# Row factors of the first block by a product, rows loaded first, and one set of weights loaded a phase earlier

## The chip, the cores and the metric

The kernel runs on one core of one Trainium2 chip. The metric is the device time of one execution in microseconds; several runs are made and their median is taken. A profile is a further execution of the same program, recorded by the hardware profiler: it has a time of its own, and a span from its first to its last instruction. The engines are named as in the profile: PE (TensorE matmuls) and PEld (its weight loads), DVE (VectorE), ACT (ScalarE), POOL (GpSimd) and SP (SyncE, which here only issues DMAs).

## The reference

One layer of a hybrid decoder, in float32, on 4096 new tokens and on 64 sample tokens (8 sequences of 8), all of width 1024:

```python
h = _rmsnorm(x, g_pre)
z = h @ w_in                       # 1024 x 2816
cb, cc, ch, cg, q, k, v, ag, mq, mg = _split_cols(z)
...                                # gated conv3 | sliding-window attention | cross-attention, each times silu(gate)
y = jnp.concatenate([out_a, out_b, out_c], axis=-1) @ w_out
return x + _rmsnorm(y, g_post), new_conv, new_k, new_v
```

with

```python
def _rmsnorm(x, g):
    xf = x.astype(jnp.float32)
    r = lax.rsqrt(jnp.mean(xf * xf, axis=-1, keepdims=True) + RMS_EPS)
    return (xf * r).astype(x.dtype) * g
```

So each token (a row of x) has one factor r. What follows is about how these factors reach the tiles that need them.

## The kernel before

**The projection.** The 4160 tokens (the 64 sample tokens first) are cut into 8 blocks of 520. The 22 groups of 128 columns of `w_in` are handled in three phases (`PHASES`): phase 0 has 8 groups as 4 pairs, phase 1 the 8 groups of the convolution, phase 2 the other 6. In the code phases count from 0; what the title of the change calls phase 1 and 2 are indices 0 and 1. A phase runs over the blocks; a block is a list of steps, and in a step PE multiplies the weights of every pair of the phase with one operand: 48 matmul instructions, each operand and weight split into a high and a low part of a reduced type (`split`, `w_split`: a cast on ACT, then a subtraction on DVE). In phase 0 the first two blocks (`PLAIN_BLOCKS`) have 8 plain steps each (`plain_block`); all later blocks have 7 steps with the sums of a Strassen-like scheme (`PRODUCTS`: A11, A12, S2, S3, S1, S4, A22 with B11, B21, T2, T3, T1, B22, T4). S1 to S4 are sums of weights, formed during blocks 3 to 6 of phase 0 and kept in DRAM (`sd`).

**Order.** Phase 0 is in an order written out by hand for all five engines, up to the first step of phase 1 (`in_order`); after that the framework's scheduler orders. In a step the jobs that belong beside it (loads, splits, sums, squares) are put between the products of its four pairs, an equal share after each: `upto = len(jobs) * (q + 1) // 4`. An engine works its instructions in order; a load waits on its queue (SP's or POOL's) until its tile is free and its source is written, and everything behind it on that queue waits too.

**The row factors.** A row tile (`nat`, 104 tokens in natural layout) is loaded by SP (`row_load`), squared and summed on ACT (`row_step`, L259); five tiles make one block. After the fifth, POOL raises the mean to the power -1/2 (L266). The operands are transposed (features on partitions, tokens along the free axis), so the factors are needed along the free axis, the same in each partition. For that POOL stores them to DRAM (`rowd`, L270), and some steps later SP loads them back, broadcast over 128 partitions (`rows_load`, L234); `row_spreads` counts the steps between. The first two blocks are multiplied without factors, and their results are scaled afterwards (`z_rows`, L597). The third block (index 2) does it another way: `rows_diag` makes five diagonal matrices of its factors (DVE, L277), `rows_product` multiplies them with a matrix of ones on PE (L286), which gives the factors in every partition, and ACT copies them out of PSUM (L288). The diagonals' tile is lent from the pool of row tiles (`rows_place`), which has two buffers; a row tile uses one of them or, early on, a slot of the weights that is still free.

**The queue of loads.** `row_queue` issues the row loads and factor loads that are due. In a plain step it comes after the step's loads of operands (`x_of`, L221); in the later steps of phase 0 (`next_block`) it comes after the loads of the next block's operands and after a sum on DVE.

**From phase 0 to phase 1.** `SWITCH` says in which step the next phase's weights are loaded (`next_loads`) and split into their slots (`next_fills`). A11, A12 and S2 are loaded and split in the last block of phase 0; S3, S1, S4 and A22 are loaded in the first steps of phase 1, into the temporary tiles (`temp`) of the new phase.

**Afterwards** come the attention, in chunks of 256 tokens (line numbers from 960 on), the output projection, and the sample tokens. `mix_s` holds the sample's mixed outputs, first written in phase 1; `pv` (L1123) holds masked weights of the window attention.

Of the kernel before, what the change touches and what calls it, by code (L numbers as in the profile page):

```python
# [8 lines left out]
F32 = mybir.dt.float32  # L9
# [3 lines left out]
ALU = mybir.AluOpType  # L13
AX = mybir.AxisListType

P = 128
D = 1024
# [3 lines left out]
NS = 64  # L21
NB = 8
NT = 4096 + NS
HW = 260
# [19 lines left out]
PLAIN_BLOCKS = 2  # L44
# [7 lines left out]
def hybrid_layer(ctx: ExitStack, tc: tile.TileContext, a: dict):  # L52
    nc = tc.nc
    TE, V, S, G, DMA = nc.tensor, nc.vector, nc.scalar, nc.gpsimd, nc.sync

    const = ctx.enter_context(tc.tile_pool(name="const", bufs=1))
    tiny = ctx.enter_context(tc.tile_pool(name="tiny", bufs=3))
# [11 lines left out]
    convw = const.tile([P, 2, 3], F32, name="convw")  # L69

    zs = const.tile([P, 14, NS], F32, name="zs")
    mix_s = const.tile([P, 8, NS], F32, name="mix_s")

    rowd = [tc.dram_tile([2 * HW], F32, name=f"rowd{b}") for b in range(NBLK)]
    hd = [{o: tc.dram_tile([P, KH, HW], F32, name=f"hd{b}_{o}") for o in ("B12", *(o for _, o in PRODUCTS))}
# [149 lines left out]
    RG = 104  # L225
# [24 lines left out]
    def row_step():  # L250

        j = sq[0]
        if j == 5 * NBLK:
            return
        b, i = divmod(j, 5)
        if i == 0:
            nat["r"] = tiny.tile([P, 8], F32, tag="r", name=f"r{b}", bufs=2)
        r, t = nat["r"], nat.pop(j)
        S.activation(t[:RG], t[:RG], AF.Square, accum_out=r[:RG, i : i + 1])  # L259
        if j in (10, 11) or j >= 14:  # L260
            row_loads.append(after_nat[0])
            after_nat[0] += 1
        sq[0] += 1
        if i == 4:
            G.tensor_scalar(r[:RG, 0:5], r[:RG, 0:5], 1.0 / D, EPS, op0=ALU.mult, op1=ALU.add)
            G.tensor_tensor(r[:RG, 0:5], r[:RG, 0:5], mhalf[:RG, 0:5], op=ALU.pow)  # L266
            if b == PLAIN_BLOCKS:
                nat["first"] = r
                return
            G.dma_start(rowd[b].rearrange("(i p) -> p i", p=RG), r[:RG, 0:5])  # L270
            row_spreads[b] = 2 if b < PLAIN_BLOCKS else 4

    def rows_diag():

        t = nat["diag"]
        for i in range(5):
            V.tensor_scalar(t[:, RG * i : RG * (i + 1)], ident[:RG, :RG], nat["first"][:RG, i : i + 1], None, op0=ALU.mult)  # L277

    def rows_place():
        nat["diag"] = natp.tile([P, D], F32, tag="nat", name="diag")[:RG, : 2 * HW]  # L280

    def rows_product():

        acc = pa2.tile([P, 2, 512], F32, tag="y", name="rows_y", bufs=2)[:, :, :HW]
        for half in range(2):
            TE.matmul(acc[:, half], ones[:RG], nat["diag"][:, HW * half : HW * half + HW], start=True, stop=True)  # L286
        rows[PLAIN_BLOCKS] = natp.tile([P, 2 * HW], F32, tag="rb", name="rb_first")
        S.copy(rows[PLAIN_BLOCKS].rearrange("p (a n) -> p a n", a=2), acc)  # L288

    def row_queue():  # L290

# [232 lines left out]
    def next_block(ph, b, p):  # L524
# [9 lines left out]
        if p < 3 and ph == 0:  # L534
            jobs.append(lambda: t_sum(ph, b, f"T{p + 2}"))
        if ph == 0:
            jobs.append(row_queue)
            if 1 <= p < 6:
                jobs.append(row_step)
        if p == 1 and nph == 1 and nb < PLAIN_BLOCKS:  # L540
# [52 lines left out]
    def z_rows(b, row):  # L593

        def one(z):
            z = z.rearrange("p a b n -> p a (b n)")
            V.tensor_tensor(z, z, rows[b].unsqueeze(1).to_broadcast([P, 2, 2 * HW]), op=ALU.mult)  # L597
        return [lambda z=zz[b][q][row]: one(z) for q in range(2)]

    def plain_jobs(b, s):  # L600
# [14 lines left out]
            (0, 4): lambda: [*parts(0, "B22"), *fills(0, "S3", "S1"), *row, *fills(0, "S4"), *row],  # L615
            (0, 5): lambda: [*sums(1, 0), *row, *sums(1, 1), *fills(1, "S2", "S3"), *row],
            (0, 6): lambda: [*parts(1, "B11"), *row, *fills(1, "S1", "S4"), *sums(3, 0), *row],
            (0, 7): lambda: [*row, *fills(3, "S2", "S3")],
            (1, 0): lambda: [*parts(1, "B21"), *z_rows(0, 1), *row, *row],
            (1, 1): lambda: [*z_rows(0, 0), *done(0, 1), *row, *row],  # L620
            (1, 2): lambda: [*parts(1, "B12"), *row, rows_place, *done(0, 0), *fills(3, "S1")],
            (1, 3): lambda: [lambda: rows_diag(), *sums(2, 0), *row],
            (1, 4): lambda: [lambda: rows_product(), *parts(1, "B22"), *sums(2, 1), *fills(2, "S2"),
                             *gains(2, "B11", "B21"), *row],
            (1, 5): lambda: [*fills(2, "S3", "S1", "S4"), *scales(2, "B11"), *row],
            (1, 6): lambda: [*gains(2, "B12"), *scales(2, "B21", "B12"), *row],
# [187 lines left out]
    def next_fills(o):  # L814
        return [lambda q=q: next_fill(1, q, o) for q in range(4)]
# [9 lines left out]
    def wo_split(j):  # L825
# [4 lines left out]
    last = NBLK - 1  # L830
    SWITCH = {(0, last - 1, 6): lambda: next_loads("A11", True),
              (0, last, 1): lambda: [*next_fills("A11"), *next_loads("A12"), *next_loads("S2", True)],
              (0, last, 3): lambda: [*next_fills("A12"), *next_fills("S2")],
              (1, 0, 0): lambda: next_loads("S3"),
              (1, 0, 1): lambda: next_loads("S1"),
              (1, 0, 2): lambda: [*next_fills("S3"), *next_loads("S4")],
              (1, 0, 3): lambda: [*next_fills("S1"), *next_loads("A22")],
              (1, 0, 4): lambda: next_fills("S4"),
              (1, 0, 5): lambda: next_fills("A22")}

    def input_projection():
        for i, (ph, b, p) in enumerate(steps):
# [135 lines left out]
    class Chunk:  # L978
# [105 lines left out]
        def window_unit(self, i, kvh, steps):  # L1084
# [34 lines left out]
            p3 = pt.rearrange("p (h q) -> p h q", h=4)  # L1119
            if not first:  # L1120

                pv = wp.tile([P, 512], F32, tag="pv", name=f"wpv{b}_{kvh}")
                G.affine_select(pv.rearrange("p (h q) -> p h q", h=4), p3, pattern=[[0, 4], [-1, P]], compare_op=ALU.is_gt,  # L1123
                                fill=0.0, base=0, channel_multiplier=1)
                steps.append((self.vts[i], pv))
# [390 lines left out]
```

## Time and profile before

| | |
|---|---|
| median of 3 runs | 1638.24 us (1634.79 to 1640.45) |
| profiled execution, its own time | 1641.21 us |
| its span | 1639.5 us |
| mean granted clock of TensorE | 0.987 |
| PE, PEld, DVE, ACT, POOL busy | 97%, 85%, 72%, 48%, 21% of the span |
| DMA | 305.89 MB, mean 187 GB/s |

How the views read: the page gives busy times of the engines and groups of instructions; the stretches view gives, for chosen times, each engine's busy time and its number of instructions, the clock granted to TensorE (1.00 is full) and the mean share of 16 DMA engines at work; the timeline lists instructions of an engine with start, duration, line, operation, tile written and tiles read, and in brackets how long the engine had been idle and what ended that; the waits view sums who waited for whom; the chain of waits is followed back from the last instruction, and its rows have a start, a duration and what ran. A row "SPq" is an instruction of SP's queue, that is a DMA being issued; the issue ends when the DMA is handed over, not when it has landed. Buffer numbers are partly left out of names: `xl5B` is an operand of block 5, `w_0S` a weight of pair 0, `c` the accumulators in PSUM, `z` the results.

### The profile page before, as it was taken

Reading aid. Unit: us, or ns where it says so; the run is one execution under the profiler, and the core shown is the slowest. Engines: PE = TensorE matmul, PEld = TensorE weight load, DVE = VectorE, ACT = ScalarE, POOL = GpSimd, SP = SyncE. Lnnn points to the kernel's source line nnn. Section 1 sums busy time; section 2 is a strip of 40 time slices with the busy share of each in tenths; the row PEclk is TensorE's granted clock in tenths of the full one; section 3 lists DMA queues with packets and bytes.
Section 4 is the critical chain, followed back from the end, with each engine's and each line's share of the span. In section 5 each row is a group of like instructions: output and inputs, shape, how many; then the busy total and the mean of one; then the engine's idle time right before and its main releaser. Section 6 shows DMA issues by size and latency. Waiting matters only on the chain.

```text
span 1639.5 us, 29607 instructions
## 1 busy us (share of the span) xinstructions
PE 1585.3 (97%) x11095; PEld 1399.6 (85%) x11095; DVE 1182.2 (72%) x2126; ACT 788.9 (48%) x2022; POOL 345.8 (21%) x590
## 2 busy tenths in 40 slices
PE   9899999999999999999999979999999999999997
PEld 9899999999999999998999955777777777777766
DVE  6578878898988777974766777666777677676733
ACT  6566655465222222443434456555555555555522
POOL 0122222220000000000000025444333443443210
PEclk9999999999999999999999989999999999999999
DMA  9979999867544333789667699666666676665152
GB/s 250 185 204 213 278 253 254 293 201 268 179 169 170 118 120 126 274 254 286 216 216 253 235 278 155 127 151 139 139 143 147 150 155 142 139 143 112 54 188 90
DMA packets 175252, 305.89 MB, mean 187 GB/s; under 512 B 31109, under 2 KB 104581, under 8 KB 175077
## 3 DMA queue, kind: packets, MB, share of 16 engines
q1 hardware_dynamic: 128213, 227.02, 44.7%
q0 software_dynamic: 46176, 75.92, 24.0%
q8 instruction: 88, 1.44, 0.4%
q10 hardware_dynamic: 720, 1.05, 0.2%
q14 instruction: 55, 0.45, 0.1%
HBM read 196.81 MB, written 108.12 MB: 186 GB/s over the span
## 4 chain that ended last, share of the span: by engine, by line
PE 49%; DVE 21%; DMA 10%; ACT 8%; issue 7%; POOL 4%; SPq 0%; ACTq 0%; DVEq 0%; POOLq 0%
PE c L345 35%; PE y L1339 6%; ACT sm L1106 5%; DMA nat<-in_x_p 3%; DVE sm L1112 3%; DVE sm L1096 2%; DVE wmx L1098 2%; PE wt L1116 2%; POOL xp L1061 1%; DVE yn L1346 1%; PE wo L976 1%; PE xs L1053 1%; DVE mix L1080 1%; DVE xr L1357 1%; DVE ml L1322 1%
## 5 line engine op out<-in xcount | busy, mean ns | idle before, releaser
L1339 PE MATMUL y<-wo,mh 128*128 128x512 f32 (+1 forms) x1072 | 351.3, 392 | 2.3 <-DVE mh L1316 1.4
L352 DVE TENSOR_TENSOR z<-c,z 128x520 f32<-128x520 f32 (+1 forms) x308 | 194.1, 645 | 83.6 <-PE c L345 82.8
L1339 PEld LDWEIGHTS y<-wo,mh 128*128 128x128 f32 x1072 | 201.0, 189 | 44.4 <-issue 4.1
L1339 PE MATMUL y<-wo,ml 128*128 128x512 f32 (+1 forms) x520 | 203.2, 391 | 1.1 <-DVE ml L1322 1.1
L1106 ACT ACTIVATE sm<-sm,wnm 128x128 f32<-128x128 f32 x256 | 99.9, 391 | 77.3 <-DVE wnm L1100 77.3
L1339 PEld LDWEIGHTS y<-wo,ml 128*128 128x128 f32 x520 | 98.5, 189 | 16.5 <-DVE ml L1322 1.6
L998 POOL DMA_DIRECT2D kst<-qd x64 | 38.9, 622 | 249.6 <-DMA qd<-z 182.4
L1123 POOL TENSOR_SCALAR_AFFINE_SELECT wpv<-wpt 128x512 f32<-128x512 f32 x62 | 39.6, 638 | 223.3 <-ACT wpt L1118 222.5
L1093 PE MATMUL ws<-kst,q 128*128 128x256 f32 x512 | 79.7, 296 | 0.5 <-ACT sm L1095 0.4
L1054 DVE TENSOR_REDUCE xmx<-xs 128x2 f32<-128x512 f32 x64 | 44.2, 690 | 42.3 <-PE xs L1053 42.2
L1057 ACT ACTIVATE xp<-xs,xnm 128x256 f32<-128x256 f32 x128 | 59.4, 469 | 31.4 <-DVE xnm L1055 25.3
L1095 ACT COPY sm<-ws 128x256 f32<-128x256 f32 x128 | 44.4, 372 | 59.2 <-PE ws L1093 56.1
L711 POOL CAST wmask<-negs 128x256 uint8<-128x256 f32 x1 | 1.4, 1419 | 324.9 <-DVE w_0S L173 324.9
L1061 POOL TENSOR_SCALAR xp<-xp,xrd 128x256 f32<-128x256 f32 x128 | 61.7, 488 | 36.6 <-DVE xrd L1058 34.0
L1347 ACT ACTIVATE y<-y 128x512 f32<-128x512 f32 (+1 forms) x66 | 38.8, 587 | 62.1 <-DVE yn L1346 62.0
L1093 PEld LDWEIGHTS ws<-kst,q 128*128 128x128 f32 x512 | 66.2, 192 | 2.4 <-ACT sm L1095 0.8
L1346 DVE TENSOR_TENSOR yn<-y,gpost 128x512 f32<-128x512 f32 (+1 forms) x66 | 45.1, 683 | 30.2 <-PE y L1339 29.8
L1357 DVE SCALAR_TENSOR_TENSOR xr<-yn,yst,xr 128x1024 f32<-128x1024 f32 (+2 forms) x34 | 42.5, 1253 | 27.9 <-POOL yst L1353 27.9
L1116 PEld LDWEIGHTS wt<-ident,sm 128*128 128x128 f32 x256 | 28.1, 144 | 38.0 <-ACT xp L1057 19.4
L259 ACT ACTIVATE nat<-nat 104x1024 f32<-104x1024 f32 x40 | 42.3, 1057 | 31.0 <-DMA nat<-in_x_p 31.0
L1066 PEld LDWEIGHTS xt<-ident,xp 128*128 128x128 f32 x256 | 29.1, 141 | 32.9 <-PE wo L976 10.5
L1116 PE MATMUL wt<-ident,sm 128*128 128x128 f32 x256 | 42.3, 289 | 15.3 <-DVE xrd L1058 8.1
(959 smaller groups left out, 5134.3 us busy)
## 6 DMA issues: line engine op xcount, KB each, us to landing
q<-qd POOLq DMA_DIRECT2D x64, 384.0 KB, 5.9
mix<-md SPq DMA_DIRECT2D x16, 1024.0 KB
xr<-in_x_p SPq DMA_DIRECT2D x32, 512.0 KB
nat<-in_x_p SPq DMA_DIRECT2D x39, 416.0 KB
o_yp<-xr SPq DMA_DIRECT2D x31, 512.0 KB
md<-th POOLq DMA_DIRECT2D x48, 260.0 KB, 6.2
qd<-zh SPq DMA_DIRECT2D x48, 260.0 KB
qd<-z SPq DMA_DIRECT2D x48, 260.0 KB
```

The source lines that it names most:

```text
L345: TE.matmul(bank[:, :HW], l, r, start=first and i == 0, stop=last and i == 3 * KH - 1)
L352: add = lambda dst, other: V.tensor_tensor(dst, c, other, op=ALU.add)
L1057: S.activation(p[:, i, :], s[:, i, :], AF.Exp, bias=nm[:, i : i + 1], scale=SCALE, accum_out=den[:, i : i + 1])
L1061: G.tensor_scalar(p[:, i, :], p[:, i, :], rd[:, i : i + 1], 0.5, op0=ALU.mult, op1=ALU.mult)
L1093: TE.matmul(s3[:, hh, :], self.q[:, 4 + 2 * (2 * half + hh) + kvh, i * P : i * P + P], self.kst[:, 2 * kvh + part, i * P : i * P + 2 * P], ...
L1095: S.copy(sm[:, 2 * half : 2 * half + 2, :], s3[:, :, P : 2 * P])
L1106: S.activation(sm[:, hh, :], sm[:, hh, :], AF.Exp, bias=nm[:, hh : hh + 1], scale=SCALE, accum_out=den[:, hh : hh + 1])
L1112: V.tensor_tensor(sm, sm, rd.unsqueeze(2).to_broadcast([P, 4, P]), op=ALU.mult)
L1116: TE.transpose(t[:, hh * P : (hh + 1) * P], sm[:, hh, :], ident)
L1339: TE.matmul(acc, self.hl[l][:, k], wo[k][c0 // 512][:, r, c0 % 512 : c0 % 512 + c1 - c0], start=j == 0, stop=j == passes * KT - 1)
L1346: V.tensor_tensor(yn[:m, c0:c1], acc[:m], gpost[:m, c0:c1], op=ALU.mult)
L1357: V.scalar_tensor_tensor(self.xr[:m, cs], yn[:m, cs], st[:m, 3:4], self.xr[:m, cs], op0=ALU.mult, op1=ALU.add)
```

## The change

Five things:

1. The first block's factors come by diagonals and a product, as the third block's do, instead of through DRAM. Their store stays, since phase 1 reads it; the first load of it goes. The second block's factors are loaded two steps later than before.
2. The diagonals lie in a tile of their own, whose place is later the sample's mix (`mix_s`), and no longer in a row tile. The row factors' small tile has three buffers instead of two.
3. In the later steps of phase 0 `row_queue` is the first job of a step.
4. S3 of phase 1 (there the fourth set of weights) is loaded and split in the last block of phase 0. S1, S4 and A22 move up by one step, loads and splits alike.
5. `pv` has two buffers instead of three.

```diff
@@ const tiles
-    mix_s = const.tile([P, 8, NS], F32, name="mix_s")
+
+    diag = const.tile([P, 2 * HW], F32, name="mix_s")
+    mix_s = diag[:, : 8 * NS].rearrange("p (k n) -> p k n", n=NS)
@@ row_step
-            nat["r"] = tiny.tile([P, 8], F32, tag="r", name=f"r{b}", bufs=2)
+            nat["r"] = tiny.tile([P, 8], F32, tag="r", name=f"r{b}", bufs=3)
...
+            if b in (0, PLAIN_BLOCKS):
+                nat["factors"] = r
             if b == PLAIN_BLOCKS:
-                nat["first"] = r
                 return
             G.dma_start(rowd[b].rearrange("(i p) -> p i", p=RG), r[:RG, 0:5])
-            row_spreads[b] = 2 if b < PLAIN_BLOCKS else 4
+            if b > 0:
+                row_spreads[b] = 4
 
     def rows_diag():
 
-        t = nat["diag"]
         for i in range(5):
-            V.tensor_scalar(t[:, RG * i : RG * (i + 1)], ident[:RG, :RG], nat["first"][:RG, i : i + 1], None, op0=ALU.mult)
-
-    def rows_place():
-        nat["diag"] = natp.tile([P, D], F32, tag="nat", name="diag")[:RG, : 2 * HW]
-
-    def rows_product():
-
-        acc = pa2.tile([P, 2, 512], F32, tag="y", name="rows_y", bufs=2)[:, :, :HW]
+            V.tensor_scalar(diag[:RG, RG * i : RG * (i + 1)], ident[:RG, :RG], nat["factors"][:RG, i : i + 1], None, op0=ALU.mult)
+
+    def rows_product(b):
+
+        acc = pa2.tile([P, 2, 512], F32, tag="y", name=f"rows_y{b}", bufs=2)[:, :, :HW]
         for half in range(2):
-            TE.matmul(acc[:, half], ones[:RG], nat["diag"][:, HW * half : HW * half + HW], start=True, stop=True)
-        rows[PLAIN_BLOCKS] = natp.tile([P, 2 * HW], F32, tag="rb", name="rb_first")
-        S.copy(rows[PLAIN_BLOCKS].rearrange("p (a n) -> p a n", a=2), acc)
+            TE.matmul(acc[:, half], ones[:RG], diag[:RG, HW * half : HW * half + HW], start=True, stop=True)
+        rows[b] = natp.tile([P, 2 * HW], F32, tag="rb", name=f"rb{b}")
+        S.copy(rows[b].rearrange("p (a n) -> p a n", a=2), acc)
@@ next_block
         if ph == 0:
-            jobs.append(row_queue)
+            jobs.insert(0, row_queue)
@@ plain_jobs
-            (0, 7): lambda: [*row, *fills(3, "S2", "S3")],
-            (1, 0): lambda: [*parts(1, "B21"), *z_rows(0, 1), *row, *row],
+            (0, 7): lambda: [lambda: rows_diag(), *row, *fills(3, "S2", "S3")],
+            (1, 0): lambda: [lambda: rows_product(0), *parts(1, "B21"), *z_rows(0, 1), *row, *row],
             (1, 1): lambda: [*z_rows(0, 0), *done(0, 1), *row, *row],
-            (1, 2): lambda: [*parts(1, "B12"), *row, rows_place, *done(0, 0), *fills(3, "S1")],
+            (1, 2): lambda: [*parts(1, "B12"), *row, *done(0, 0), *fills(3, "S1")],
             (1, 3): lambda: [lambda: rows_diag(), *sums(2, 0), *row],
-            (1, 4): lambda: [lambda: rows_product(), *parts(1, "B22"), *sums(2, 1), *fills(2, "S2"),
+            (1, 4): lambda: [lambda: rows_product(2), *parts(1, "B22"), *sums(2, 1), *fills(2, "S2"),
@@ SWITCH
-              (0, last, 3): lambda: [*next_fills("A12"), *next_fills("S2")],
-              (1, 0, 0): lambda: next_loads("S3"),
-              (1, 0, 1): lambda: next_loads("S1"),
-              (1, 0, 2): lambda: [*next_fills("S3"), *next_loads("S4")],
-              (1, 0, 3): lambda: [*next_fills("S1"), *next_loads("A22")],
-              (1, 0, 4): lambda: next_fills("S4"),
-              (1, 0, 5): lambda: next_fills("A22")}
+              (0, last, 3): lambda: [*next_fills("A12"), *next_fills("S2"), *next_loads("S3")],
+              (0, last, 5): lambda: next_fills("S3"),
+              (1, 0, 0): lambda: next_loads("S1"),
+              (1, 0, 1): lambda: next_loads("S4"),
+              (1, 0, 2): lambda: [*next_fills("S1"), *next_loads("A22")],
+              (1, 0, 3): lambda: next_fills("S4"),
+              (1, 0, 4): lambda: next_fills("A22")}
@@ window_unit
-                pv = wp.tile([P, 512], F32, tag="pv", name=f"wpv{b}_{kvh}")
+                pv = wp.tile([P, 512], F32, tag="pv", name=f"wpv{b}_{kvh}", bufs=2)
```

## The prediction

> **What bounds the kernel now.** I read the page first, then the stretches table (PE against the other engines, with granted clock and DMA), then the timelines of SP, ScalarE and VectorE where PE stood still, and the chain of waits.
>
> ```profile
> span 1639.5 us, 29607 instructions
> PE 1585.3 (97%) x11095; PEld 1399.6 (85%) x11095; DVE 1182.2 (72%) x2126; ACT 788.9 (48%) x2022; POOL 345.8 (21%) x590
> ```
>
> PE is busy for 97% of the span, so nothing can come of work taken off the other engines as such; only PE's own holes and PE's slow clock can be won. 54 us are not busy in all. The stretches of 10 us show where the holes of the changed stages lie. Columns: PE, PEld, DVE, ACT, POOL busy (x instructions), granted clock, DMA share, GB/s.
>
> ```profile
> 50.00:60.00 10.00, 10.00 (x86) 10.00 (x85) 6.71 (x12) 5.98 (x14) 2.88 (x3) 1.00 0.88 108
> 60.00:70.00 10.00, 10.00 (x86) 10.00 (x86) 5.88 (x7) 4.83 (x11) 0.00 (x0) 1.00 0.75 122
> 70.00:80.00 10.00, 6.62 (x56) 6.41 (x54) 3.52 (x10) 3.81 (x9) 2.23 (x4) 1.00 1.04 277
> 80.00:90.00 10.00, 5.12 (x22) 4.67 (x23) 5.31 (x14) 7.75 (x16) 4.14 (x7) 0.76 1.01 270
> 90.00:100.00 10.00, 10.00 (x78) 10.00 (x78) 8.32 (x15) 8.34 (x19) 0.00 (x0) 0.90 0.62 157
> 220.00:230.00 10.00, 9.85 (x81) 9.47 (x79) 5.66 (x9) 3.72 (x7) 1.61 (x3) 1.00 1.00 246
> 230.00:240.00 10.00, 8.31 (x57) 8.29 (x57) 7.61 (x10) 8.13 (x18) 4.85 (x8) 0.83 0.98 234
> 270.00:280.00 10.00, 9.17 (x77) 8.96 (x75) 7.84 (x9) 9.73 (x22) 4.67 (x7) 1.00 0.84 231
> 350.00:360.00 10.00, 10.00 (x85) 10.00 (x85) 9.69 (x12) 7.82 (x16) 1.08 (x2) 1.00 0.28 108
> 370.00:380.00 10.00, 9.45 (x79) 9.24 (x78) 5.55 (x6) 3.51 (x6) 0.32 (x1) 1.00 0.82 302
> 380.00:390.00 10.00, 8.02 (x53) 7.79 (x54) 8.24 (x12) 5.74 (x10) 0.00 (x0) 0.83 1.00 352
> ```
>
> At full rate PE does 86 products in 10 us, 0.116 us each. From 70 to 100 it does 56 + 22 + 78 = 156 of 258: 102 lost, 11.9 us. From 220 to 240 it does 138 of 172: 4.0 us lost; from 270 to 280, 77 of 86: 1.0 us; from 370 to 390, 132 of 172: 4.7 us. These 21.6 us are what this change can reach; the rest of the span is left as it is.
>
> Where the largest hole comes from, back from PE: first timeline rows (start, duration, engine, line, operation, tiles; in brackets the idle time before and what ended it), then two rows of SP's waits (total, times, longest), last a row of the chain.
>
> ```profile
> 81.66 0.54 PE L345 MATMUL c<-hi_1B,w_0A 128*128 128x260 f32 x1 [5.05 <-ACT z L659]
> 87.79 1.32 PE L286 MATMUL rows_y<-diag,ones 104*128 104x260 f32 x4 [3.21 <-DVE diag L277]
> 81.04 0.57 ACT L659 COPY z<-c 128x520 f32<-128x520 f32 x1
> 79.98 1.06 ACT L259 ACTIVATE nat<-nat 104x1024 f32<-104x1024 f32 x1 [4.58 <-DMA nat<-in_x_p]
> 87.01 1.01 DVE L277 TENSOR_SCALAR diag<-ident,r 104x104 f32<-104x104 f32 x5 [1.01 <-ACT nat L259]
> 58.34 1.73 ACT L561 ACTIVATE hi_1B<-xl1B,gpre 128x260 fp32r<-128x260 f32 x4 [2.93 <-DMA xl1B<-in_xt]
> 64.70 4.70 DVE L597 TENSOR_TENSOR z<-z,rb 128x1040 f32<-128x1040 f32 x4 [4.12 <-DMA rb<-rowd]
> 45.18 0.65 SPq L221 DMA_DIRECT2D xl1B<-in_xt  x1
> 56.22 0.35 SPq L234 DMA_DIRECT2D rb<-rowd  x1
> 56.66 1.04 SPq L248 DMA_DIRECT2D nat<-in_x_p  x2
> 61.18 8.86 SPq L248 DMA_DIRECT2D nat<-in_x_p  x2
> SPq L234 <- DMA rowd<-r: 10.3, 1, 10.3
> SPq L248 <- PE rows_y L286: 6.6, 1, 6.6
> 42.39 13.81 DMA rowd<-r
> ```
>
> PE stood 5.05 us for a PSUM copy on ScalarE; that copy stood behind the squares of a row tile (nat) that landed only at 79.98; the loads stood behind SP, which from 45.83 to 56.22 did nothing but wait for the first block's factors (rowd) to reach memory, 13.81 us for 2 KB. Then PE stood 3.21 us for the third block's diagonals, because their tile, lent from the row tiles, had to wait for another square (1.01).
>
> **Part by part. A, the first block's factors by a product, diagonals in their own tile.** Gone: the load rb<-rowd of the first block, and with it SP's wait of 10.3 us. The store rowd<-r stays (it is read again in the second phase). Behind SP's wait stood the row tiles of 56.66, the second block's last operand, the third block's first and the row tiles of 61.18: the first four can go some 10 us earlier; the tiles of 61.18 still wait for the squares that follow the split of 58.34, so they are not issued earlier, but find less queued ahead of them. Gone too is the lent tile, so the wait of 1.01 on DVE and SP's 6.6 us on the product. One more thing moves: with one job less in its step, the squares of the tile that landed at 79.98 come after that step's first PSUM copy on ScalarE, not before it.
>
> Added: 5 diagonals on DVE (1.01 in the row of 87.01, in a stretch, 50:60, where DVE has 3.3 us of 10 free), one product on PE and one PSUM copy on ACT. The copy lies ahead of the split of 58.34, before which ACT idles 2.93 us: free. The product is on the path: the row of 87.79 has 1.32 us, between half and full clock; 0.7 to 1.3, I take 1.0. DVE's scaling of 64.70 loses its wait of 4.12, which brings the gates forward on ACT.
>
> The hole is 11.9 us: 5.05 + 3.21 idle, and 24% + 10% of two stretches at lower clock, 3.4, which agrees (11.7). What is late next is the row tile issued at 61.18: 61.18 + 8.86 is where its pair was out, 70.04, and 79.98 where it had landed. If it needs 10 us from 61.2 it is there at 71 to 72, about when its step wants it; I leave 1.4 us for that. A = -11.9 + 1.0 + 1.4 = -9.5. Bounds -11.2 and, if that tile lands no earlier, -3.9 (below).
>
> The second block's factor load moves two steps later, from (1, 1) to (1, 3); it is first used in (1, 7), so it costs nothing. Its cover is four steps of 5.6 us (48 products each).
>
> **B, rows first in a step.** In the blocks that still take squares, the row tile's load is put ahead of the loads of the next block's operands:
>
> ```profile
> 211.43 5.63 SPq L221 DMA_DIRECT2D xl5B<-in_xt  x4
> 217.16 1.03 SPq L248 DMA_DIRECT2D nat<-in_x_p  x1
> 225.86 1.06 ACT L259 ACTIVATE nat<-nat 104x1024 f32<-104x1024 f32 x1 [6.77 <-DMA nat<-in_x_p]
> 231.71 0.42 PE L345 MATMUL c<-lo_4T,w_0A 128*128 128x260 f32 x1 [1.69 <-DVE lo_4T L336]
> 232.92 3.32 ACT L308 ACTIVATE xl5B<-xl5B,gpre 128x260 f32<-128x260 f32 x8
> ```
>
> The row tile could have been issued at 211.43, was at 217.16, and ACT waited 6.77 us for it; the split behind it reached PE 1.69 us late and the clock fell. 5.7 us earlier covers that hole (4.0 us) and the one at 270 (1.0). The operands go about 0.4 us later, one issue; they are first used at 232.92. Bounds -5.0 and 0; since the tile has the weights' four loads just ahead of it either way, I take -4.5.
>
> **Clock.** The row of 230:240 has a clock of 0.83 after an idle of 1.69 us, so a short hole costs some 1.7 us more: 17% of 10. [...]
>
> **C, the fourth weights (S3) of the second phase loaded in the first.** Now, two rows of the chain and then of the timelines:
>
> ```profile
> 369.78 7.86 DMA vd<-v
> 377.79 3.23 DMA wr_0S<-sd0S
> 381.11 0.62 ACT L169 CAST w_0S<-wr_0S 128x512 fp32r<-128x512 f32 x1 [6.01 <-DMA wr_0S<-sd0S]
> 385.34 0.68 DVE L173 TENSOR_TENSOR w_3S<-wr_3S,w_3S 128x512 fp32r<-128x512 f32 x1
> 381.78 0.39 PE L345 MATMUL c<-hi_0T,w_0S 128*128 128x260 f32 x1 [2.34 <-ACT w_0S L169]
> ```
>
> The weights' room is free only when the store vd<-v has landed; ACT waits 6.01 us, PE 2.34 and then runs at a lower clock (0.83 in 380:390). Moved, the four loads use the quiet DMA of 350:360 (0.28) and PE finds the weights: up to -4.7. The four casts (0.62) and four subtractions (0.68) now fall in the last block, where DVE is 97% busy: 0 to 2.7 us late for PE, and 1.7 more if the clock falls. I take 1.5, since DVE has 4.4 us free at 370:380 to catch up. The next weights (S1) then come first behind the same vd<-v, needed a step (5.6 us) later: the first is there at 381.0, and split at 382.3, while PE wants it at 381.78 - 2.34 + 5.6 = 385.0. C = -3.2.
>
> **Costed at nothing.** The attention's pv tile has two buffers for three:
>
> ```profile
> 1415.29 0.63 POOL L1123 TENSOR_SCALAR_AFFINE_SELECT wpv<-wpt 128x512 f32<-128x512 f32 x1
> 1417.74 1.08 PE L976 MATMUL wo<-wpv,vt 128*64 128x512 f32 x4
> 1431.69 0.63 POOL L1123 TENSOR_SCALAR_AFFINE_SELECT wpv<-wpt 128x512 f32<-128x512 f32 x1 [3.60 <-ACT wpt L1118]
> ```
>
> A pair is read 12.9 us before the next one is written. The third r tile and the longer mix tile move no work.
>
> **Sum.** -9.5 - 4.5 - 3.2 = -17.2. The profiled execution took 1641.2 us (span 1639.5 and 1.7 around it), 3.0 over the median of the runs, 1638.2. So 1624.0 against its own time, and 1621.0 as the median.
>
> **Rivals.** (1) The DMA engines are full, and what is issued earlier lands no earlier. For it: shares of 0.75 to 1.04 from 50 to 80. Against: at 50:70 only 108 and 122 GB/s moved, while SP waited, against 277 after. Then the 5.05 us and one slow window of 1.7 stay, 3.21 + 1.7 go, the product costs 1.0: A = -3.9, B = 0, C = -3.2: 1631. [...] (2) The fills in the last block cost as much as they save: 2.7 + 1.7 = 4.4, C = -0.3: 1624. (3) Slower: the row tile put first waits for its slot, and the operands wait behind it in SP's queue. In four blocks a whole step would be lost, 5.6 + 1.7 = 7.3 each, 29 us: B = +29, 1655. It decides once that wait exceeds what the operands have in hand: issued by 217.1, used at 232.9, some 10 us for the transfer (the row tile of 217.16 took 8.7), so from 5 to 6 us on. Against: at 211.43 the load had nothing left to wait for. (4) The waits only change hands: ScalarE still reaches its copies late because its split of 58.34 waits for the same transfer, and each gain is taken back in the same block: -2, 1636.
>
> **How the numbers follow.** Chances: forecast 0.55, (1) 0.15, (2) 0.15, (3) 0.07, (4) 0.08. About 0.3%, 4.9 us, is what a measurement of this kernel can tell from no change. Faster by more: the forecast, (2) and most of (1), 0.82; within it (4) and a little of (1), 0.10; slower (3), 0.08. The forecast's own best is -11.2 - 5.0 - 4.7 = -20.9, 1617; allowing 1 us for the spread of the runs, the low end is 1616. The high end takes in rival (1), 1632; left out are (3) and (4).
>
> **What would show it.** SP issues the row tiles of 56.66 near 46 and never waits for rowd in the first 60 us. No idle of PE over 2 us between 70 and 95, granted clock 1.00 there; rows_y x8 instead of x4. ACT's wait of 6.77 us for nat near block four is under 3. PE does not wait for w_0S at the start of phase two. Wrong would be: the square at 79.98 still waiting about 4 us for its tile; PE waiting over 2 us for lo or z in the last block of phase one; xl operands late behind nat.

## The result and the profile after

| | before | after | ratio, 95% interval |
|---|---|---|---|
| first comparison, median | 1638.24 us (7 runs) | 1625.98 us (7 runs) | 0.9929 (0.9913 to 0.9944) |
| second comparison, another chip | 1637.93 us (22 runs) | 1627.92 us (9 runs) | 0.9932 (0.9908 to 0.9956) |
| profiled execution of the first | 1641.21 us | 1625.52 us | |

The change makes the kernel 0.7% faster: 12.3 us in the first comparison, 10.0 in the second. Forecast were 17.2, a median of 1621.0 with 1616 to 1632 around it. Direction and range held; the sum was some 5 to 7 us too large, and the question of the experiments was which terms.

The page of the changed kernel:

```profile
span 1623.8 us, 29613 instructions
PE 1579.5 (97%) x11099; PEld 1395.2 (86%) x11099; DVE 1182.6 (73%) x2131; ACT 790.8 (49%) x2023; POOL 345.8 (21%) x590
```

Its stretches of 10 us, with the columns of the table of before:

```profile
70.00:80.00 10.00, 10.00 (x83) 9.91 (x81) 5.42 (x14) 6.65 (x13) 4.14 (x7) 1.00 1.05 323
80.00:90.00 10.00, 10.00 (x86) 9.97 (x85) 7.93 (x14) 8.71 (x20) 0.00 (x0) 1.00 0.82 225
90.00:100.00 10.00, 10.00 (x85) 10.00 (x84) 5.54 (x6) 6.80 (x14) 1.61 (x3) 1.00 0.74 253
110.00:120.00 10.00, 8.96 (x73) 8.55 (x72) 7.95 (x11) 4.33 (x7) 3.78 (x7) 1.00 0.83 165
120.00:130.00 10.00, 8.05 (x52) 7.64 (x52) 8.52 (x11) 4.60 (x7) 0.00 (x0) 0.83 0.87 251
220.00:230.00 10.00, 10.00 (x86) 10.00 (x85) 9.28 (x11) 9.05 (x19) 5.40 (x9) 1.00 1.08 297
230.00:240.00 10.00, 10.00 (x86) 10.00 (x85) 8.69 (x12) 6.13 (x11) 3.81 (x8) 1.00 0.95 251
270.00:280.00 10.00, 10.00 (x86) 10.00 (x85) 8.87 (x11) 5.23 (x9) 3.48 (x7) 1.00 0.96 287
370.00:380.00 10.00, 8.34 (x70) 8.13 (x69) 9.40 (x14) 8.86 (x14) 0.00 (x0) 1.00 0.96 350
380.00:390.00 10.00, 9.88 (x83) 9.67 (x82) 10.00 (x14) 7.05 (x16) 0.00 (x0) 1.00 0.61 202
```

The hole at 70 to 100 is gone: 254 products of 258, where it was 156. So are those at 220 to 240 and at 270. At 370 to 390, 153 products stand against 132. But from 110 to 130 there is a hole that the prediction did not have: 125 of 172, and a clock of 0.83.

The steps behind it, in the timelines of SP, PE and ScalarE:

```profile
43.68 3.62 SPq L250 DMA_DIRECT2D nat<-in_x_p  x2
59.58 1.37 SPq L250 DMA_DIRECT2D nat<-in_x_p  x2
55.23 1.04 PE L286 MATMUL rows_y<-mix_s,ones 104*128 104x260 f32 x4
70.65 1.06 ACT L261 ACTIVATE nat<-nat 104x1024 f32<-104x1024 f32 x1 [0.81 <-DMA nat<-in_x_p]
79.18 1.04 PE L286 MATMUL rows_y<-mix_s,ones 104*128 104x260 f32 x4
219.44 1.06 ACT L261 ACTIVATE nat<-nat 104x1024 f32<-104x1024 f32 x1 [1.49 <-DMA nat<-in_x_p]
121.76 0.39 PE L345 MATMUL c<-hi_2T,w_0S 128*128 128x260 f32 x1 [1.06 <-ACT hi_2T L335]
123.04 0.39 PE L345 MATMUL c<-lo_2T,w_0S 128*128 128x260 f32 x1 [0.89 <-DVE lo_2T L336]
376.15 0.39 PE L345 MATMUL c<-lo_0T,w_0S 128*128 128x260 f32 x1 [1.66 <-DVE lo_0T L336]
```

The row tiles issued at 56.66 go out at 43.68 and 46.97, the two products take 1.04 us each without idle time ahead of them, the square near block four waits 1.49 us where it waited 6.77, and at the start of phase two PE no longer waits for w_0S, but 1.66 us for lo_0T. The rows at 121.76 and 123.04 are the new hole.

**Where PE gains and loses.** For each kernel the start of the same product of the projection can be compared with its start in the profile of before. The differences by stage, in us (positive is gained), from one profile each:

| profile | first hole, 53 to 95 | third block, 112 to 137 | fourth to sixth block, 137 to 281 | phase switch, 356 to 466 |
|---|---|---|---|---|
| after | 10.5 | -3.1 | 5.1 | 1.6 |
| after, second profile | 8.7 | -3.0 | 5.1 | 1.1 |

After 466 us up to the end of the projection the sum changes by less than 1 us, but for the start of phase three (670 to 730), which loses 1.2 in both. Through the attention (967 to 1554) it stays within 0.5 us. At 1554 us the first profile is 13.1 us ahead, at its end 15.7. The rest falls into the last 70 us, where the profile of before has 15 us at a clock of 0.66 and that of after 20 us at 0.83; no part of the change reaches there. The medians lie only 12.3 apart: the profiled execution of before was 3.0 us longer than its median.

### The profile page after: what moved, and what is told of

Its sections match the earlier page's. It is cut to its first block, busy times and chain, and to the rows that moved or that the text cites. A ratio compares the mean times of both kernels' runs of the same rounds, so it can differ in the third digit from the quotient of the medians.

```text
span 1623.8 us, 29613 instructions
## 1 busy us (share of the span) xinstructions
PE 1579.5 (97%) x11099; PEld 1395.2 (86%) x11099; DVE 1182.6 (73%) x2131; ACT 790.8 (49%) x2023; POOL 345.8 (21%) x590
## 4 chain that ended last, share of the span: by engine, by line
PE 65%; DVE 17%; ACT 6%; issue 5%; DMA 4%; POOL 3%; SPq 0%; ACTq 0%; POOLq 0%; DVEq 0%
PE c L345 45%; PE y L1339 10%; ACT sm L1106 4%; DVE sm L1112 2%; PE wo L976 2%; PE wt L1116 2%; DVE sm L1096 2%; PE ws L1093 2%; DVE wmx L1098 1%; PE xs L1053 1%; POOL xp L1061 1%; PE xo L976 1%; PE xt L1066 1%; DVE xr L1357 1%; DVE ml L1322 1%
## 5 line engine op out<-in xcount | busy, mean ns | idle before, releaser
L1066 PEld LDWEIGHTS xt<-ident,xp 128*128 128x128 f32 x256 | 29.1, 141 | 33.0 <-PE wo L976 10.5
L1118 ACT COPY wpt<-wt 128x512 f32<-128x512 f32 x64 | 36.9, 577 | 39.2 <-PE wt L1116 38.5
```

The source lines that it names most:

```text
L1066: TE.transpose(t[:, i * P : (i + 1) * P], p[:, i, kt * P : (kt + 1) * P], ident)
```

## Experiments

The profile of before is one execution. Each of the twelve kernels below has the code of before or that of the changed kernel in some stages, so its profile is a further look at those too. The gains by stage are put together behind the experiments. Times are medians, and a ratio is to the kernel before on the same chip, with its 95% interval; a gain in us is worked out from the ratio, and can differ by a microsecond or so from the difference of the medians.

### One part at a time

**Part A alone.** The change with the queue last again, as below, and with the `SWITCH` of before:

```diff
-            jobs.insert(0, row_queue)
+            jobs.append(row_queue)
...
```

> Only part A: the first block's factors by a product, diagonals in their own tile; rows last in a step and S3 in the second phase as before. If A alone makes the gain of the first 100 us and also what is given back in the third block (stores moved up into the landing time of a factor store), PE is some 10.4 us ahead at 100 us and about 7 ahead at 140: 1638.2 - 7 = about 1631. If what is given back comes from rows being first (part B), it is not given back here: 1628. By the prediction's sum, A = -9.5: 1628.7.

Measured: 1633.6 against 1642.52 us, 0.9953 (0.993 to 0.9977), that is -7.7 us by the ratio. Its ten runs reach from 1627 to 1641. The profiled one took 1639.1 and still has a hole. ScalarE and PE in the timeline, then the stretch:

```profile
69.79 1.06 ACT L261 ACTIVATE nat<-nat 104x1024 f32<-104x1024 f32 x1 [4.84 <-DMA nat<-in_x_p]
77.39 1.06 ACT L261 ACTIVATE nat<-nat 104x1024 f32<-104x1024 f32 x1 [4.35 <-DMA nat<-in_x_p]
83.61 2.07 PE L286 MATMUL rows_y<-mix_s,ones 104*128 104x260 f32 x4 [3.34 <-DVE mix_s L280]
```

```profile
80.00:90.00 10.00, 6.66 (x30) 6.10 (x29) 7.21 (x18) 6.16 (x15) 2.88 (x6) 0.66 1.01 307
```

Row tiles issued at 49.54 and 60.50 landed at 69.8 and 77.4; the diagonals came late, and PE waited 3.34 us and its clock fell to 0.66 in the stretch. So in this execution A left half of the hole, although its times say that the kernel gains; other profiles with A, below, have it closed. The third block loses nothing here against before: what the changed kernel gives back there is not A's alone.

**Part B alone.** The kernel before with one line changed:

```diff
-            jobs.append(row_queue)
+            jobs.insert(0, row_queue)
```

> Only part B: the kernel before with the row loads first in each later step. If B is independent of A, the waits near 231 and 275 us go and nothing else moves: -4.5 by the prediction, -5.1 by the two profiles: 1633 to 1634. If B was only possible because A had freed the queues, or if B is what costs 3 us in the third block: -2 or less, 1636.

Measured: 1639.74, 0.9988 (0.9972 to 1.0004), -2.0 us. The waits near 231 and 275 are gone in the stretches, and the timeline of PE has a new one:

```profile
220.00:230.00 10.00, 10.00 (x86) 10.00 (x85) 7.34 (x12) 4.79 (x8) 1.61 (x3) 1.00 1.03 266
230.00:240.00 10.00, 10.00 (x86) 10.00 (x85) 8.76 (x11) 8.20 (x18) 5.12 (x8) 1.00 1.03 334
```

```profile
131.97 0.58 PE L345 MATMUL c<-hi_2T,w_0S 128*128 128x260 f32 x1 [2.29 <-ACT hi_2T L335]
```

That row is the other half: in the third block PE now waits 2.29 us, and this profile loses 5.2 us there. B makes its gain, 4.7 us by this profile, and has paid as much a hundred microseconds earlier.

**Part C alone.** The kernel before with the `SWITCH` of the change.

> Only part C: S3 loaded and split in the last block of the first phase, S1, S4 and A22 a step earlier. By the prediction -3.2: 1635. If the fills, and the S1 weights that now come too late for DVE, cost nearly as much as the saved wait (the two profiles: -0.8 to -2.3): 1636 to 1637.5, with PE idle for a lo or hi tile in the last block and of about 1.8 us in the fifth step of the second phase. If C costs more than it saves: over 1638.5.

Measured: 1639.27, 0.9979 (0.9957 to 1.0002), -3.4 us with an interval that holds everything from 0 to 7. Its profile gains 1.1 us at the phase switch.

**SP let go, without the product.** The kernel before, and:

```diff
-            row_spreads[b] = 2 if b < PLAIN_BLOCKS else 4
+            row_spreads[b] = 3 if b == 0 else 2 if b < PLAIN_BLOCKS else 4
```

> The kernel before with one number changed: the first block's factors are loaded back one step later (3 instead of 2), behind that step's two row tiles and operand. No product, no other tile for the diagonals. If the 10.3 us that SP stood in its queue were the cause of the 5 us hole, the loads that stood behind are issued some 10 us earlier and most of A comes without the product: -5 to -8 (the lent diagonals' tile still costs its 3.2): 1630 to 1633. If the first block's scaling on DVE (which waited 4.1 us for these factors) was the cause, it waits as long or longer: 0 to +2, 1638 to 1640.

Measured: 1642.38, 0.9998 (0.998 to 1.0015): nothing. SP issues the row tiles at 43.58 and 46.85, as in the changed kernel, but ScalarE then stands for the first block's scaling, which needs the factors that now come later:

```profile
66.98 1.79 ACT L405 ACTIVATE th<-z 128x520 f32<-128x520 f32 x3 [8.34 <-DVE z L597]
```

Before, that wait was 3.83. Its profile, of the shortest of ten runs, does gain 6.9 us in the first hole: PE's wait of 5.05 us is gone there, and one of 2.75 us remains in front of the third block's product, whose diagonals still lie in a lent tile:

```profile
80.96 1.95 PE L286 MATMUL rows_y<-diag,ones 104*128 104x260 f32 x4 [2.75 <-DVE diag L277]
```

The median says that this is not the usual run, and no profile shows where the others lose it. So letting SP go gains nothing in the time by itself. Part A has two things more, the factors early and a tile of its own for the diagonals; no run takes these two apart.

### The third block

The chain backwards in the changed kernel: PE waits 1.06 and 0.89 us at 121.76 and 123.04; ScalarE stood until 117.44 for a temporary tile, which the gates' store md<-th gave back when it landed; and that store ran behind a 520 KB store hd_B<-xl2B and the factors' store.

**The sum in its old place.** DVE's order showed that the queue, put first, had moved the sum of operands behind an accumulation:

```diff
-            jobs.insert(0, row_queue)
+            jobs.insert(1 if p in (1, 2) else 0, row_queue)
```

> The changed kernel, but in the second and third step of a block, where no operands are loaded, the sum of operands (DVE) comes ahead of the row queue again, as before the change; in the other steps rows stay first. Theory: putting the queue first moved that sum one job later, behind the step's accumulation on DVE (seen in the third block of both kernels with part B, not in those without), so that the low part of the next operand reached PE late. Then the waits of 1.06 and 0.89 us at 121.8 and 123.0 and the half-clock stretch behind them go, 3 us in the third block, and PE gains nothing elsewhere: -3 us or a little more against the changed kernel. Rival: the third block is late because the temporary tiles come free late from stores that stand behind the factors' store; then the order of the sum changes nothing: 0.

Measured: 1629.85, 0.9946 (0.9929 to 0.9962), no gain over the changed kernel. In its third block it still loses 2.7 us; PE's wait for hi_2T falls from 1.06 to 0.64. By these two profiles the place of the sum is worth 0.4 us; as the main cause the theory fell.

**The factors' store on another queue.**

```diff
-            G.dma_start(rowd[b].rearrange("(i p) -> p i", p=RG), r[:RG, 0:5])
+            put = lambda q: q.dma_start(rowd[b].rearrange("(i p) -> p i", p=RG), r[:RG, 0:5])
+            if b == 3:
+                late.append(lambda: put(S))
+            else:
+                put(G)
```

> The changed kernel, with one store moved: the fourth block's factors (520 elements of 4 bytes, issued at 106.1 by POOL, landed at 116.3) go out on ScalarE's queue at the start of the next step. The rival of the third block's loss: the gates' stores behind it on POOL's queue (issued at 108.0, landed at 117.4) keep a temporary tile, for which ScalarE waits from 115.0 to 117.4. By it those stores land in about 5 us, ScalarE's wait goes and 2 to 3 us of the third block come back. By the theory of the sum's place, at most the 0.9 us that DVE waited there: -1 to 0.

Measured: 1629.71, 0.9949 (0.9932 to 0.9966), no gain over the changed kernel. ScalarE's wait for the tile falls to 0.61, and in the step where the changed kernel loses 3.1 us this profile loses 0.6. But the edit costs something itself, a step earlier:

```profile
106.93 0.58 ACTq L273 DMA_DIRECT2D rowd<-r  x1
109.94 0.39 PE L349 MATMUL c<-lo_2B,w_0A 128*128 128x260 f32 x1 [0.89 <-DVE lo_2B L340]
```

The store's issue on ScalarE waits until POOL has the factors, at 106.90. The cast of hi_2B stands behind it and starts at 107.55, where the changed kernel has it at 102.62; PE waits for the low part, and 1.4 us are lost there and 0.3 in the next step, 2.3 in all. The gates' stores also go out later, at 110.79 instead of 108.00, and the first of them still takes 7.7 us with nothing of the factors ahead of it; the 520 KB store ahead of it on the same queue still takes 10.5. So the factors' store does not make that one long; whether it is part of the third block's loss this run cannot say.

**Rows first only where operands are loaded in pairs.**

```diff
-            jobs.insert(0, row_queue)
+            jobs.insert(0 if p >= 3 else len(jobs), row_queue)
```

> The changed kernel, with the row queue first only in the steps 3 to 6 of a block, where three operands are loaded; in the steps 0 to 2 it stays last. Theory: in the third block's first step the row tile put first waits for its buffer until the square before it is done, and the 520 KB operand behind it is issued 4.4 us later, together with a 520 KB store; that store then takes 10 to 12 us instead of 5, the stores behind it land late, ScalarE waits 2.1 to 2.5 us for a temporary tile, and PE 1.1 and 0.9 us in the step after. Then the operand is issued ahead of the row tile, the store takes about 5 us again, the third block loses nothing against the kernel before, and the gains of the fifth and sixth block stay: 2 to 3 us faster than the changed kernel. Rival: part B's gain near 231 us comes from the first step too, and goes with it: 0, or slower.

Measured: 1627.91 us, 0.9931 (0.9906 to 0.9955), against 1627.92 of the changed kernel on the same chip: no gain in time. In its profile, though, the third block loses nothing and the later gain stays whole (5.0 us). The timelines of SP and ScalarE in the changed kernel, then the view of DMA issues for the 520 KB store in them (KB, median us from issue to landing):

```profile
97.77 4.81 SPq L250 DMA_DIRECT2D nat<-in_x_p  x2
102.67 0.39 SPq L223 DMA_DIRECT2D xl3B<-in_xt  x1
117.44 0.63 ACT L386 CAST zh<-z 128x520 fp32r<-128x520 f32 x1 [2.38 <-DMA md<-th]
```

```profile
hd_B<-xl2B POOLq DMA_DIRECT2D x1, 520.0 KB, 9.8
```

and the same two views of the kernel with rows first from step 3 on:

```profile
107.38 0.39 SPq L223 DMA_DIRECT2D xl3B<-in_xt  x1
111.48 0.32 SPq L250 DMA_DIRECT2D nat<-in_x_p  x1
124.65 0.63 ACT L386 CAST zh<-z 128x520 fp32r<-128x520 f32 x1 [0.37 <-DMA md<-th]
```

```profile
hd_B<-xl2B POOLq DMA_DIRECT2D x1, 520.0 KB, 5.1
```

In the first, two row tiles go first; the second of them waits for its buffer until 102.3, the operand behind it leaves at 102.67, and 0.11 us later (102.78) POOL issues a store of the same size. In the other, the operand leaves 4.1 us ahead of the row tile and 4.6 ahead of the store (111.99). The store takes 9.8 us in one and 5.1 in the other, and ScalarE's wait goes from 2.38 to 0.37. But this profile is one with its first hole open, so PE was 9 us later here than in the changed kernel; the kernel with an earlier sum, below, suggests that this matters.

**The complement.** The kernel before, with the queue ahead of the operand in the first step alone:

```diff
-            jobs.append(row_queue)
+            jobs.insert(0 if p == 0 else len(jobs), row_queue)
```

> The kernel before, with the row queue ahead of the operand load in the first step of a block alone (the other steps as before). This is the complement: by the theory of the colliding load and store it has the third block's loss (3 to 5 us, with the 520 KB store at 10 to 12 us) and none of part B's gains near 231 and 275 us: 2 to 4 us slower than the kernel before. If part B's gain comes from the first steps, it is as fast or faster than before.

Measured: 1639.28, 1.0009 (0.9988 to 1.0029). The store takes 11.4 us and ScalarE waits 2.04, as expected; but PE loses 0.7 us in the third block, not 3 to 5, and no slowdown can be seen in the time. Of B's later gain, 1.3 us are there against about 5.

### The changed kernel again, and with an earlier sum

> The changed kernel once more, on the same chip as the three beside it, for the comparison with them and a second profile. By the first runs 0.991 to 0.994 of the kernel before. Its third block loses about 3 us and the first step of the third phase 0 to 3; how far the first hole (70 to 100 us) is closed may differ from the first profile, by when the row tiles land.

Measured: 0.9932, as in the table at the top; its profile agrees with the first stage by stage.

**Sum ahead of the S1 fills.** Rows first from step 3 on, and in the third step of phase two:

```diff
-                jobs = SWITCH[ph, b, p]() + jobs
+                n = 1 if (ph, b, p) == (1, 0, 2) else 0
+                jobs = jobs[:n] + SWITCH[ph, b, p]() + jobs[n:]
```

> As the kernel with the queue first from step 3 on, and in the third step of the second phase the sum of operands (DVE) is put ahead of the S1 fills. Theory of the 1.8 us wait for lo_0T at 374: DVE does two of S1's subtractions, the sum and a third subtraction before the split PE waits for, while it idled 4.5 us just before. Then the sum falls into that idle time and the wait shrinks by 1.2 us or more: 1 to 2 us better than its neighbour. Rival: the split waits for ScalarE's high part, which is late because of the weights' casts; then nothing changes.

DVE in the changed kernel, then DVE, PE and ScalarE in this one, and its store in the view of DMA issues:

```profile
372.51 0.68 DVE L175 TENSOR_TENSOR w_2S<-wr_2S,w_2S 128x512 fp32r<-128x512 f32 x1
373.11 1.23 DVE L325 TENSOR_TENSOR xl0B<-xl0B,x_0T 128x1040 f32<-128x1040 f32 x1
374.26 0.68 DVE L175 TENSOR_TENSOR w_3S<-wr_3S,w_3S 128x512 fp32r<-128x512 f32 x1
374.86 1.23 DVE L336 TENSOR_TENSOR lo_0T<-x_0T,hi_0T 128x1040 fp32r<-128x1040 f32 x1
```

```profile
366.92 1.23 DVE L325 TENSOR_TENSOR xl0B<-xl0B,x_0T 128x1040 f32<-128x1040 f32 x1
373.75 0.69 DVE L175 TENSOR_TENSOR w_2S<-wr_2S,w_2S 128x512 fp32r<-128x512 f32 x1
374.72 1.24 DVE L336 TENSOR_TENSOR lo_0T<-x_0T,hi_0T 128x1040 fp32r<-128x1040 f32 x1 [0.27 <-ACT hi_0T L335]
376.02 0.39 PE L345 MATMUL c<-lo_0T,w_0S 128*128 128x260 f32 x1 [0.86 <-DVE lo_0T L336]
118.70 0.63 ACT L386 CAST zh<-z 128x520 fp32r<-128x520 f32 x1 [3.33 <-DMA md<-th]
```

```profile
hd_B<-xl2B POOLq DMA_DIRECT2D x1, 520.0 KB, 12.1
```

The sum falls into idle time, the split comes right behind the subtraction for w_2S, and the step loses 1.1 us instead of 2.0 to 2.9 in the six profiles with the fills as in the change. The steps behind it lose 0.8 us where the others gain 0.3, and the time is the same: 1628.79, 0.9934 (0.991 to 0.9958). The row of 118.70 and the store are a miss for the theory of the third block: here the operand went out 4.1 us ahead of the row tile (98.47 and 102.57), and the store still took 12.1 us. In this execution the first hole was closed, and three more 520 KB stores had gone out at 95.35, 96.50 and 97.42, the last of them 1.1 us ahead of the operand; in the profile with the 5.1 they lay at 101.14 to 103.21, 4.2 us ahead.

### The phase switch

**The changed kernel without C.** `SWITCH` as before.

> The changed kernel without part C (S3 loaded and split in the second phase as before). The difference to the changed kernel is C in the presence of A and B: by the prediction 3.2 us, by the first profiles 1 to 2. PE idles about 2.3 us for w_0S at the start of the second phase and runs at half clock behind it. If C is worth nothing, the two are the same within a microsecond.

Measured: 1627.51, 0.9938 (0.9915 to 0.996). All three parts gave 0.9929 and 0.9932, so C is about 1 us here, less than these intervals can tell. PE waits for w_0S again, 1.65 us.

**S3 alone early**, the other loads and fills in their old steps:

```diff
-              (1, 0, 0): lambda: next_loads("S1"),
-              (1, 0, 1): lambda: next_loads("S4"),
-              (1, 0, 2): lambda: [*next_fills("S1"), *next_loads("A22")],
-              (1, 0, 3): lambda: next_fills("S4"),
-              (1, 0, 4): lambda: next_fills("A22")}
+              (1, 0, 1): lambda: next_loads("S1"),
+              (1, 0, 2): lambda: next_loads("S4"),
+              (1, 0, 3): lambda: [*next_fills("S1"), *next_loads("A22")],
+              (1, 0, 4): lambda: next_fills("S4"),
+              (1, 0, 5): lambda: next_fills("A22")}
```

> The changed kernel, with S3 alone moved into the last block; S1, S4 and A22 are loaded and split in the steps of before the change. If the 1.8 us wait for lo_0T at 374 comes from S1's subtractions standing ahead of the split on DVE one step early, it goes, and 1 to 2 us are won. If S1 is then late in its own step (as the fills were before the change), the wait moves to about 380 and nothing is won; over 2 us worse if PE's clock falls there.

Measured: 1628.37, 0.9941 (0.9918 to 0.9963). The wait at 374 is gone, but two steps later 4.4 us are lost:

```profile
384.38 0.51 ACT L308 ACTIVATE xl1B<-xl1B,gpre 128x260 f32<-128x260 f32 x1 [5.04 <-DMA xl1B<-in_xt]
386.41 0.39 PE L345 MATMUL c<-hi_0T,w_0A 128*128 128x260 f32 x1 [1.74 <-ACT w_0A L171]
```

The next block's operand, issued behind the later weights, holds ScalarE 5.04 us, and its casts come late. The second reading held: the wait moved. Of the two, the change's order is the better one by 2 us in the profiles.

## Why the prediction was right, and where its sum was off

Stage means over all profiles that have a part against those without it (first hole: nine with A, four without; fourth to sixth block: nine with B's steps 3 to 6, four with none of B; phase switch: six with C as in the change, six without). Each profile is one execution, so these are estimates; their sum comes near the measured time:

| term | predicted | stage means |
|---|---|---|
| A, first hole | -9.5 | -7.8 with, -2.1 without: -5.7 |
| B, fourth to sixth block | -4.5 | -4.7 with, +1.5 without: -6.2 |
| third block | 0 | +2.7 in the eight with rows first in the first step |
| C, phase switch | -3.2 | -1.0 with, +0.3 without: -1.3 |
| sum | -17.2 | -10.5 (medians: -12.3 and -10.0) |

That the time still came out within the forecast range owes something to luck: A and C were taken too large and the third block's loss was left out, but B gained more than forecast. (One of the nine profiles with B, that of the sum in its old place, loses 2.3 us more right at 281 us, on the edge of the stage; with them the nine are at -4.5.)

**A was mis-sized because its base was one execution.** The mechanism came as described: SP free, row tiles out ten microseconds earlier, the product at 1.04 us where 1.0 was taken, diagonals without a lent tile. But "the hole is 11.9 us" was true of that profile only. Three other kernels with the same code there lost 94, 67 and 73 products of 258 between 70 and 100 us, where the profile of before lost 102: 10.9, 7.8 and 8.5 us, so 9.8 in the mean. And with A six of nine profiles lose 0.5 to 1.3 us, but three still lose 4.4 to 7.6. The step that failed is the allowance of 1.4 us for the row tile issued at 61.18: in those three ScalarE waits 4.4 to 5.0 us for that tile (4.35 above), which the prediction itself had named as the sign of being wrong. What decides when that tile lands no run shows. One thing goes with it: SP's second load of the third block's operand left by 53.8 us in the six profiles with the hole closed, and at 55.2 to 57.2 in the three others. The chain that the prediction drew is also not shown as far as it went: it took SP's wait as the cause of the 5.05 us, and the run with SP free but the factors no earlier gained nothing in the time.

**B's mechanism was right, its gain larger than thought and its price left out.** ScalarE's wait of 6.77 is 1.49, and the gain in the later blocks, 6.2 us between the means, is above the bound of 5.0, since the other profiles without B had lost more there than the profile of before. What the prediction missed is that the same line also acts in the first step of a block. It had the mechanism, as rival (3): a row tile put first waits for its buffer, with the operand behind it. That happens, in the third block, by 4 us; but the price is not the whole step (5.6 us, and 29 with the clock in four blocks) that the rival put on the operand's lateness. It is 2.7 us in the mean, and what goes with it in all eight profiles is that the operand's load leaves 0.1 us ahead of a store of its size, which then takes 9.8 to 12.0 us. That this meeting is the cause is likely but not shown (see what is left open). The rival was looked for in the step where the gain was, and was ruled out there with the right row; the first step was not looked at.

**C was priced at its own wait, not at the next.** The wait for w_0S and its slow clock go: 4.0 us gained, where 4.7 was the bound. In the last block the fills cost 0.7 us, where 1.5 was taken. The step that failed is the one on S1, which compared its landing and first split (381.0 and 382.3) with PE's need (385.0). It is there in time, but its subtractions and a sum stand on DVE ahead of the split PE needs first, and PE waits 1.66 us for lo_0T (2.0 to 2.9 us lost in the six profiles). The prediction named each engine's free time in that stretch (4.4 us on DVE) but not the order in it; the kernel with an earlier sum shows that the order was a large part of it: the wait is 0.86 and 1.1 us are lost.

**Costed at nothing:** the attention's pv tile. From 967 to 1554 us the profiles move against that of before by -1.3 to +1.4 us with two buffers (nine of them) and by -1.3 to +0.4 with three (four): no difference that can be told.

**Left open:** why the 520 KB store takes 5 us in some executions and 10 to 12 in others. Rows first in the first step, with the operand beside it, gives the long one in all eight profiles; without that, five of six have the short one, and the sixth has the three other stores close by. So it is more than one order on one queue. The five short ones also all come from profiles in which PE was less than 7 us ahead of before at 112 us, and the sixth was 9.8 ahead; no profile has the first hole closed and the short store. Nor does the long store have one price: 0.7 us in the complement, 5.2 with part B alone. And neither of the two kernels that remove that order is measurably faster. The start of phase three loses 1.2 us in both profiles of the changed kernel, and in the others anything from 3.2 lost to 1.0 gained, with no part that it goes with. None of the versions beat the changed kernel.

## What to carry to other kernels

A hole in one profile is a sample: when what closes it is the landing of a DMA, look at the same code in several executions before its length becomes a term of a sum; here it lost 11.9, 10.9, 7.8 and 8.5 us in four profiles. When a queue's order is changed by one line that acts in many steps, look at every step where the moved load can wait for its buffer, and at what else is issued at the moment it then leaves; here that was a store of the same size, which took 9.8 us, and 5.1 in the profile where the load left 4.6 us ahead of it. And when a wait on an engine goes, the next instruction in that engine's order is a candidate for the next wait, even where the engine has free time in the stretch: here PE's 2.34 us for w_0S went and 1.66 us for lo_0T came, with 4.4 us of 10 free on DVE before the change.

## What the runs showed of the hardware

**The same store, 5 or 12 us.** Over all fourteen profiles the fourth operand store of the third block (520 KB) took 4.9 to 5.2 us in five and 9.8 to 12.1 in nine. All that took the short time lost nothing in that block against before; those that took the long time lost 0.7 to 5.2 us. In eight of the nine a load of 520 KB was issued 0.1 us ahead of the store. Whether what is issued on one queue makes a store on another take longer the runs do not show: with the factors' store on ScalarE's queue the first of the gates' stores still took 7.7 us, but the long 520 KB store, 10.5 us, was still ahead of it on its own queue.

**In these profiles the length of one idle time does not settle the clock.** After 1.69 us (before, at 231.71) and after 1.06 and 0.89 us close together (after, at 121.76 and 123.04) the clock fell to 0.83 of the stretch. After a single 1.66 us (after, at 376.15) it stayed at 1.00, and so it did after 2.09 us in the second profile of the changed kernel, in PE's timeline and then in the stretches:

```profile
378.25 0.39 PE L345 MATMUL c<-lo_0T,w_0S 128*128 128x260 f32 x1 [2.09 <-DVE lo_0T L336]
```

```profile
370.00:380.00 10.00, 7.91 (x66) 7.70 (x65) 7.31 (x11) 6.88 (x11) 0.00 (x0) 1.00 0.98 335
380.00:390.00 10.00, 10.00 (x84) 9.82 (x82) 10.00 (x15) 6.83 (x15) 0.00 (x0) 1.00 0.69 230
```

The 1.7 us that the prediction put on every short hole is therefore paid in some and not in others. What decides between the two no run shows.
